# Summing the gathered v rows of a PEER expert layer on TensorE in four 32-column tiles instead of on VectorE

## The chip, the core and the metric

The kernel runs on one core of one Trainium2 chip. The metric is the device time of one execution in microseconds (us). A core has TensorE (PE in the profile, with its weight loads as PEld), VectorE (DVE), ScalarE (ACT), GpSimd (POOL) and SyncE (SP), which issues most transfers. PSUM is the memory that TensorE writes into, in eight banks.

## The reference

One decoder layer on 512 tokens of 1024 channels: a gated mixer of a short convolution and a differential attention, a cross-attention to 256 positions, and then the part that matters here, product-key expert retrieval (PEER): each token and head picks 16 of 16,384 experts, each expert being one row u and one row v.

```python
def chunk(hc):                                     # PEER_HEADS 8, PEER_TOPK 16
    ...
    g = jax.nn.softmax(top_s, axis=-1)
    ue = peer_u[experts]
    ve = peer_v[experts]
    act = jax.nn.gelu(jnp.einsum('td,thkd->thk', hc, ue).astype(jnp.float32), approximate=False)
    return jnp.einsum('thk,thkd->td', (g * act).astype(ve.dtype), ve)
...
x = x + peer_ffn(hf, w_pq[l], sub_keys[l], peer_u[l], peer_v[l])
return rmsnorm(x, final_g)
```

So each token has 128 chosen experts (8 heads by 16), here called its slots.

## The kernel before

Most products run as three float32r passes over a two-part split (hi by hi, hi by lo, lo by hi; `product`, L120). The expert layer takes tokens in two ways. The last 384 tokens (the dense ones) are multiplied with all 16,384 experts, 128 experts to a block j: `stage_u` forms a block's activations (24 matmuls of 384 columns, L120, then a Gelu on ScalarE, L695), and a step of `experts` sums a block up (18 matmuls of 512 columns, L750, into six PSUM banks that stay taken to the end). The first 128 tokens take only the rows they chose: `gathered` fetches rows with an indirect transfer, a token on each partition, so that "row" s is slot s of all 128 tokens (512 KB). Rows 0 to 127 are of u: VectorE multiplies each with the token's normed channels and sums up (L801), which gives the slots' weights `wx`. Rows 128 to 255 are of v: VectorE adds each, times its weight, to `acc` (L812).

The order of the work is set by the loop of `experts` over j = 0 to 127 and by a scheduler that orders the instructions of each engine ahead of time. Steps 85 to 116 hold a `stage_u` as well; steps after that and before it hold only the sum. At the end of each step the loop tells the generator `gathered` how many rows to issue: about one in a step without an activation, three in a step with one, none in the last two. The rows that one step issues are used up in the next. So the v rows begin in step 64, and 96 of the 128 fall to the 32 steps with an activation.

What a step's rows hang on:

- the index column of each row is copied by VectorE into a small tile `now` (L798) that takes its turn with the tiles of tag "e"; before, the row's weight is copied there too (L808);
- the transfer is issued by GpSimd (L818) into one of seven row buffers (four in "res", two "oh", one "row");
- SyncE's queue loads the blocks of u and v for the dense tokens (L108, L733).

At the end the four blocks of tokens get the residual, the norm and the write (L764 to L772); block 0 is the gathered one, with `acc` in SBUF.

Of the kernel before, what the change touches and what calls it, by code (L numbers as in the profile page):

```python
"""Hybrid block on one core: gated short conv + differential attention, memory cross-attention, PEER.

Activations are channel-major ([channel, token]) up to the expert layer. Every float32 product runs
as three float32r passes over exact two-part splits (hi*hi + hi*lo + lo*hi). The expert layer takes
the first 128 tokens by gathering the rows they chose, and the other 384 against all experts on the
tensor engine, with the gates laid out densely.
"""
# [7 lines left out]
F32 = mybir.dt.float32  # L15
F32R = mybir.dt.float32r
BF16 = mybir.dt.bfloat16
I32 = mybir.dt.int32
# [5 lines left out]
P = 128  # L24
# [17 lines left out]
# the order of the work  # L42
EARLY = 5  # convolution channels kept beside the chunks
LAG = 1  # heads before the first convolution channels
SOON = 5  # memory weights loaded ahead of the input
PROLOGUE = 96  # blocks of experts activated before the first is summed up
BY_HEAD = 5  # of them, by each head's choice of experts
BY_BLOCK = 3  # and by each block of tokens' gates
FILL = 4  # and at the end of the gates
AHEAD = 11  # blocks activated ahead of the sum after that  # L50
NA = 3  # one-hot rows of four that ScalarE makes
MM = 1  # gate banks taken from the products
X_HEAD = 4  # gathered rows by two heads' choice
X_BLOCK = 3  # and by each block of tokens' gates
XW = 3  # rows in a step with an activation, to one in a step without
LAST = 2  # steps without rows at the end
LAST_J = 2  # blocks summed up token block by token block at the end
# [4 lines left out]
class Block:  # L62
    # tag: (pool, slots)
    TAGS = {
# [26 lines left out]
    def rows(self, name):  # L91
        """a vector on every partition"""
        src = self.a[name]
        return bass.AP(tensor=src.tensor, offset=src.offset, ap=[[0, P], [1, D]])

# [18 lines left out]
    def product(self, out, w, x):  # L114
        """out[c, t] = sum over d of w[d, c] x[d, t]"""
        whi, wlo = w
        for k in range(KC):
            xhi, xlo = x[0][k], x[1][k]
            for p, (ww, xx) in enumerate(((whi, xhi), (whi, xlo), (wlo, xhi))):
                self.nc.tensor.matmul(out, ww[:, k, :], xx, start=(k == 0 and p == 0), stop=(k == KC - 1 and p == 2))  # L120
# [17 lines left out]
    def roots(self, out, acc, n, inv, eps, log=False, bank="tr"):  # L138
        """out[t, i] = 1 / sqrt(inv * sum of squares + eps) of token 128 i + t; acc holds sums by partition"""
# [7 lines left out]
    def inverse_root(self, out, ss, inv, eps, log=False):  # L147
        """1 / sqrt(ss * inv + eps). By log: exp(-log / 2), and a Newton step, where ScalarE holds that table; else three
        Newton steps from the exponent halved in the bits"""
# [16 lines left out]
    def spread(self, r, n, bank="tr"):  # L166
        """the tokens' values along the free dim, on every partition (in PSUM)"""
# [24 lines left out]
    def parameters(self):  # L192
        nc, a, m = self.nc, self.a, self.misc
        nc.vector.tensor_scalar(out=self.g_sub, in0=self.small[:, 56:57], scalar1=1.0 - LAM_INIT, scalar2=None, op0=ALU.mult)
        # lambda = exp(q1.k1) - exp(q2.k2) + init, the same on every partition
# [9 lines left out]
        # relative bias by distance, reversed: entry e stands for distance 511 - e  # L205
# [36 lines left out]
    def diff_head(self, h, x):  # L242
# [4 lines left out]
        # each component's 64 channels on both halves of the partitions: queries as (hi, lo), keys as (hi, hi)  # L247
# [21 lines left out]
        for pair in range(2):  # L269
            # weights of two query blocks, two key blocks to a tile  # L270
            ahi = [self.t("aw", [P, 2, 2 * P], F32R) for _ in range(pair + 1)]
            alo = [self.t("aw", [P, 2, 2 * P], F32R) for _ in range(pair + 1)]
            for qi in range(2):
# [24 lines left out]
                for b in range(pair + 1):  # L298
# [3 lines left out]
                    if m == 1:  # L302
                        # this key block is all in the future of the pair's first query block
# [32 lines left out]
    def gated(self, sg, w_out, y, gate, x):  # L336
        """sigmoid(gate projection) * (y @ w_out)"""
# [7 lines left out]
    def add_and_scale(self, w, y, res, g):  # L345
        """res += y @ w, in place; returns the split of res * g, and the sums of squares by partition"""
# [19 lines left out]
    def memory(self):  # L366
        """keys and values of the cross-attention, to DRAM: the products need no norm, which scales the positions"""
# [5 lines left out]
        # some weights ahead of the input, which the norm needs as a whole  # L373
# [50 lines left out]
    def mem_keys(self):  # L424
        """channel-major: [channel, position] by chunk"""
# [8 lines left out]
    def mem_values(self):  # L434
        """token-major: [position, part, position block, channel] by chunk"""
# [62 lines left out]
    def keys_scores(self, h, x, yk, xk):  # L498
        """the best 16 keys of each half, for the dense and for the gathered tokens"""
# [15 lines left out]
    def keys_pairs(self, n, vals, idx, ei, ej, ez):  # L515
        """the best 16 sums of one from each half, for n pairs of a head and a block of tokens: rows, columns, sums less the largest"""
# [420 lines left out]
```

## Time and profile before

| | |
|---|---|
| runs of the kernel before | 2159.32 and 2159.57 us, median 2159.45 |
| span of the profiled execution, first to last instruction | 2152.3 us |
| the profiled execution's own time | not recorded apart from its span; the runs are 7.1 us above the span |
| TensorE busy | 2048.0 us, 95% of the span |
| VectorE busy | 1505.0 us, 70% |
| ScalarE busy | 1004.1 us, 47% |
| bytes moved | 440.09 MB, mean 204 GB/s |

The span is cut below into the stretches that matter: from 1714.6 us (step 64, the first v rows) to 1808.7 (step 85), to 1848.8 (step 90), to 2084.4 (step 118), to 2129.5 (step 127), and to the end. The borders are starts of L739, which each step has once on VectorE. Matmuls overlap one another in the trace, so their cost is read from the distance of their starts, not from their durations.

### The profile page before, as it was taken

Reading aid. Unit: us, or ns where it says so; the run is one execution under the profiler, and the core shown is the slowest. Engines: PE = TensorE matmul, PEld = TensorE weight load, DVE = VectorE, ACT = ScalarE, POOL = GpSimd, SP = SyncE. Lnnn points to the kernel's source line nnn. Section 1 sums busy time; section 2 is a strip of 40 time slices with the busy share of each in tenths; the row PEclk is TensorE's granted clock in tenths of the full one; section 3 lists DMA queues with packets and bytes.
Section 4 is the critical chain, followed back from the end, with each engine's and each line's share of the span. In section 5 each row is a group of like instructions: output and inputs, shape, how many; then the busy total and the mean of one; then the engine's idle time right before and its main releaser. Section 6 shows DMA issues by size and latency. Waiting matters only on the chain.

```text
span 2152.3 us, 29167 instructions
## 1 busy us (share of the span) xinstructions
PE 2048.0 (95%) x10341; PEld 1772.6 (82%) x10341; DVE 1505.0 (70%) x3531; ACT 1004.1 (47%) x1716; POOL 341.4 (16%) x301
## 2 busy tenths in 40 slices
PE   7499999999999999999998999999999999999997
PEld 6477877788887878899898989988777877888985
DVE  5356565642345568999887777557887887887897
ACT  5244444432233344343369999953333333333332
POOL 1000000000000000001231111012222234564431
PEclk9799999999999999999999999999999999999999
DMA  7532222223433124246687777589999988899984
GB/s 219 135 98 74 74 85 78 69 88 98 145 110 100 60 78 127 87 129 219 206 281 273 266 279 244 194 299 307 350 321 333 340 310 276 312 357 352 350 298 157
DMA packets 162787, 440.09 MB, mean 204 GB/s; under 512 B 15185, under 2 KB 70497, under 8 KB 160593
## 3 DMA queue, kind: packets, MB, share of 16 engines
q1 hardware_dynamic: 124464, 300.98, 41.7%
q0 software_dynamic: 38176, 137.25, 18.6%
q8 instruction: 81, 1.33, 0.2%
q14 instruction: 66, 0.53, 0.1%
HBM read 391.50 MB, written 46.66 MB: 204 GB/s over the span
## 4 chain that ended last, share of the span: by engine, by line
PE 51%; DMA 13%; DVE 13%; ACT 12%; issue 7%; POOL 2%; another core or an unknown queue 2%; SPq 0%; ACTq 0%; DVEq 0%; POOLq 0%
PE psmm L120 30%; PE psmm L750 5%; ACT slot L858 5%; PE pslg L120 5%; PE pstr L750 4%; DVE lo L99 3%; DMA raw<-in_peer_v 3%; DMA res<-in_peer_v,e 3%; ACT sq L850 3%; DMA act<-sp 2%; ACT hi L98 2%; PE pspv L750 2%; DMA res<-in_peer_u,e 1%; DMA res<-in_peer_u,kp 1%
## 5 line engine op out<-in xcount | busy, mean ns | idle before, releaser
L98 ACT ACTIVATE hi<-raw 128x1024 fp32r<-128x1024 f32 x388 | 410.9, 1061 | 633.0 <-PE psmm L120 288.4
L99 DVE TENSOR_TENSOR lo<-raw,hi 128x1024 fp32r<-128x1024 f32 x388 | 472.7, 1220 | 302.4 <-ACT hi L98 296.1
L120 PE MATMUL psmm<-A,hi 128*128 128x512 f32 x1408 | 451.1, 397 | 1.9 <-DVE Yb L450 1.9
L120 PE MATMUL psmm<-n,hi 128*128 128x384 f32 x1472 | 391.4, 343 | 1.2 <-ACT sp L695 1.2
L120 PEld LDWEIGHTS psmm<-A,hi 128*128 128x128 f32 x1408 | 262.3, 188 | 60.0 <-issue 4.2
L120 PE MATMUL psmm<-A,lo 128*128 128x512 f32 x704 | 280.6, 399 | 0.0
L120 PEld LDWEIGHTS psmm<-n,hi 128*128 128x128 f32 x1472 | 266.7, 188 | 1.6 <-ACT sp L695 1.5
L120 PE MATMUL psmm<-n,lo 128*128 128x384 f32 x736 | 251.6, 342 | 4.7 <-DVE lo L99 4.5
L818 POOL DMA_INDIRECT res<-in_peer_u,e x85 | 94.1, 1107 | 453.9 <-DVE e L798 430.2
L120 PEld LDWEIGHTS psmm<-A,lo 128*128 128x128 f32 x704 | 132.7, 189 | 28.6 <-issue 2.0
L98 ACT ACTIVATE tr<-e 128x384 fp32r<-128x384 f32 x128 | 66.6, 520 | 182.9 <-DVE e L739 179.0
L120 PE MATMUL pslg<-n,hi 128*128 128x384 f32 x576 | 148.3, 338 | 0.0
L120 PEld LDWEIGHTS psmm<-n,lo 128*128 128x128 f32 x736 | 138.3, 188 | 8.2 <-DVE lo L99 7.9
L750 PE MATMUL psmm<-hi,tr 128*128 128x512 f32 x384 | 129.0, 400 | 15.5 <-ACT tr L98 8.5
L801 DVE CUSTOM_DVE_ANT_0 res<-res,hx 128x1024 f32<-128x1024 f32 x101 | 122.5, 1219 | 24.8 <-DMA res<-in_peer_u,e 16.9
L750 PE MATMUL psmm<-lo,tr 128*128 128x512 f32 x384 | 131.1, 396 | 0.3 <-DVE lo L99 0.3
L818 POOL DMA_INDIRECT res<-in_peer_v,e x74 | 103.7, 1401 | 125.2 <-DVE e L808 103.1
L750 PE MATMUL psmm<-hi,e 128*128 128x512 f32 x384 | 119.6, 397 | 1.7 <-DVE e L798 1.6
L818 POOL DMA_INDIRECT res<-in_peer_u,kp x16 | 20.4, 1274 | 616.5 <-DVE kp L798 552.7
L120 PEld LDWEIGHTS pslg<-n,hi 128*128 128x128 f32 x576 | 105.3, 188 | 3.1
L856 DVE TENSOR_SCALAR oh<-iota,e 128x128 f32<-128x128 f32 x384 | 106.8, 345 | 0.0
L812 DVE SCALAR_TENSOR_TENSOR acc<-res,e,acc 128x1024 f32<-128x1024 f32 x73 | 93.5, 1281 | 15.8 <-DMA res<-in_peer_v,e 15.6
(299 smaller groups left out, 3748.2 us busy)
## 6 DMA issues: line engine op xcount, KB each, us to landing
raw<-in_uT SPq DMA_DIRECT2D x128, 512.0 KB, 4.5
raw<-in_peer_v SPq DMA_DIRECT2D x128, 512.0 KB, 5.9
raw<-in_w_in SPq DMA_DIRECT2D x64, 512.0 KB, 3.5
gates<-slot SPq DMA_DIRECT2D x16, 1536.0 KB, 6.7
slot<-gates SPq DMA_DIRECT2D x16, 1536.0 KB, 12.2
act<-sp SPq DMA_DIRECT2D x64, 192.0 KB, 3.8
raw<-in_w_pq SPq DMA_DIRECT2D x16, 512.0 KB, 3.5
raw<-in_w_ckv SPq DMA_DIRECT2D x12, 512.0 KB, 7.5
```

The lines of the kernel that those rows point to most:

```text
L98: self.nc.scalar.activation(hi, src, AF.Copy)
L99: self.nc.vector.tensor_tensor(out=lo, in0=src, in1=hi.bitcast(F32), op=ALU.subtract)
L120: self.nc.tensor.matmul(out, ww[:, k, :], xx, start=(k == 0 and p == 0), stop=(k == KC - 1 and p == 2))
L750: nc.tensor.matmul(accs[2 * i + half], l[:, ts], m[:, half * 512 : half * 512 + 512], start=(jj == 0 and p == 0), stop=(jj == NK - 1 and p ...
L801: nc.vector.tensor_tensor_reduce(out=t, in0=t, in1=hx, op0=ALU.mult, op1=ALU.add, scale=1.0, scalar=0.0, accum_out=wx[:, 0, s : s + 1])
L812: nc.vector.scalar_tensor_tensor(out=acc, in0=t, scalar=w, in1=acc, op0=ALU.mult, op1=ALU.add)
L818: nc.gpsimd.indirect_dma_start(out=t, out_offset=None, in_=a["peer_u"] if s < P else a["peer_v"], in_offset=bass.IndirectOffsetOnAxis(ap=i ...
L850: nc.scalar.activation(sq[:, w, :], self.iota, AF.Square, bias=it[:, t0 + w : t0 + w + 1], scale=-1.0)
L856: nc.vector.tensor_scalar(out=oh[:, 4 + w, :], in0=self.iota, scalar1=cols[:, 0, t - b * TB : t - b * TB + 1], scalar2=cols[:, 1, t - b * ...
L858: nc.scalar.copy(stage[:, :, q * 4 : q * 4 + 4].rearrange("p j w -> p w j"), pp.rearrange("p (w j) -> p w j", w=4))
```

## The change

The 128 v rows are fetched by token: row 128 + k now holds, on partition s, the v row of slot s of token k. The expert indices are transposed once for that (`ext`). The sum over the slots becomes a sum over partitions, so a matmul can do it: for token k the stationary operand is a 128 x 32 block that holds the token's 128 weights in column k mod 32 and zeros elsewhere (`wd`, a tile of 32 such blocks, whose diagonals VectorE refreshes once for each 32 tokens), and the moving operand is a quarter of the row, 256 channels. Quarter q goes to PSUM partitions 32 q to 32 q + 31, so the four matmuls of a token use four column tiles, 32 columns wide, of the array. All operands are float32. 32 tokens accumulate in one bank of tag "lg", which ScalarE then copies to `acc`. The result lies by quarters (partition 32 q + k mod 32), and `gathered_out` finishes block 0 in that layout. The row buffers are six instead of seven, since the buffer "row" now holds `wd`. The change also strips comments, which is left out here.

```diff
-        wx = self.t("wx", [P, 2, P])
-        ex = self.t("ex", [P, P], I32)
-        acc = self.accx = self.t("acc", [P, D])
-        nc.vector.scalar_tensor_tensor(out=ex, in0=xi, scalar=float(NK), in1=xj, op0=ALU.mult, op1=ALU.add)
+        wx = self.t("wx", [P, P])
+        ex, exf = self.t("ex", [P, P], I32), self.t("wt", [P, P])
+        acc = self.accx = self.t("acc", [P, NT, 256])
+        nc.vector.scalar_tensor_tensor(out=exf, in0=xi, scalar=float(NK), in1=xj, op0=ALU.mult, op1=ALU.add)
+        nc.vector.tensor_copy(ex, exf)
+        pt = self.ps("tr")[:, :P]
+        nc.tensor.transpose(pt, exf, self.ident)
+        ext = self.t("xt", [P, P], I32)
+        nc.vector.tensor_copy(ext, pt)
...
-                    nc.vector.tensor_copy(now[:, s - done : s - done + m], ex[:, s % P : s % P + m])
+                    nc.vector.tensor_copy(now[:, s - done : s - done + m], (ex if s < P else ext)[:, s % P : s % P + m])
...
                 else:
-                    w = fl[:, k : k + 1]
-                    nc.vector.tensor_copy(w, wx[:, 1, s - P : s - P + 1])
-                    if s == P:
-                        nc.vector.tensor_scalar(out=acc, in0=t, scalar1=w, scalar2=None, op0=ALU.mult)
-                    else:
-                        nc.vector.scalar_tensor_tensor(out=acc, in0=t, scalar=w, in1=acc, op0=ALU.mult, op1=ALU.add)
+                    k = s - P
+                    b, r = divmod(k, 32)
+                    if wt is None:
+                        wd = self.t("row", [P, 32, 32])
+                        nc.gpsimd.memset(wd, 0.0)
+                        diag = bass.AP(tensor=wd.tensor, offset=wd.offset, ap=[list(wd.ap[0]), [33, 32]])
+                        pt = self.ps("lg")[:, :P]
+                        nc.tensor.transpose(pt, wx, self.ident)
+                        wt = self.t("wt", [P, P])
+                        nc.scalar.copy(wt, pt)
+                    if r == 0:
+                        nc.vector.tensor_copy(diag, wt[:, k : k + 32])
+                        pv = self.ps("lg")[:, :256]
+                    for q in range(4):
+                        nc.tensor.matmul(pv[32 * q : 32 * q + 32, :], wd[:, r, :], t[:, 256 * q : 256 * q + 256], start=(r == 0), stop=(r == 31))
+                    if r == 31:
+                        nc.scalar.copy(acc[:, b, :], pv)
...
-        for i in range(NT):
+        self.gathered_out(fin)
+        for i in range(1, NT):
...
+    def gathered_out(self, fin):
+        nc, a = self.nc, self.a
+        quarters = lambda dram, q: dram.rearrange("(b r) d -> r b d", r=32)[:, :, 256 * q : 256 * q + 256]
+        acc = self.accx
+        xt = self.t("raw", [P, NT, 256])
+        fg = self.t("row", [P, 256])
+        src = a["final_g"]
+        for q in range(4):
+            qs = slice(32 * q, 32 * q + 32)
+            nc.sync.dma_start(out=xt[qs], in_=quarters(self.x3[0], q))
+            nc.sync.dma_start(out=fg[qs], in_=bass.AP(tensor=src.tensor, offset=src.offset + 256 * q, ap=[[0, 32], [1, 256]]))
+        nc.vector.tensor_tensor(out=xt, in0=xt, in1=acc, op=ALU.add)
+        nc.scalar.activation(acc, xt, AF.Square)
+        ss = self.t("sq", [P, 8])
+        nc.vector.tensor_reduce(out=ss[:, 0:4], in_=acc, op=ALU.add, axis=AX.X)
+        quads = self.t("oh", [P, P])
+        nc.sync.dma_start(out=quads, in_=a["quads"])
+        pt = self.ps("lg")[:, :4]
+        nc.tensor.matmul(pt, quads, ss[:, 0:4], start=True, stop=True)
+        self.inverse_root(fin, pt, 1.0 / D, EPS)
+        for b in range(NT):
+            nc.vector.scalar_tensor_tensor(out=xt[:, b], in0=xt[:, b], scalar=fin[:, b : b + 1], in1=fg, op0=ALU.mult, op1=ALU.mult)
+        for q in range(4):
+            nc.sync.dma_start(out=quarters(a["out"][0], q), in_=xt[32 * q : 32 * q + 32])
...
-        self.tags = ("oh", "oh", "row")
+        self.tags = ("oh", "oh")
```

The order of the instructions on TensorE in a step with an activation, where its product (L120) ends and its sum (L750) begins. `pslg` is the bank of the product, `psmm` one of the six banks of the sum. Before:

```order
L120 MATMUL pslg_17409<-n_6485,hi_17412 128x384
L120 MATMUL pslg_17409<-n_6486,hi_17412 128x384
L120 MATMUL pslg_17409<-n_6485,lo_17413 128x384
L750 MATMUL psmm_13138<-hi_17444,tr_17450 128x512
L750 MATMUL psmm_13139<-hi_17444,tr_17450 128x512
```

And in the changed kernel, in such a step (`row` is `wd`; `oh` and `res` are row buffers; `pslg_17476` is the bank of the 32 tokens):

```order
L120 MATMUL pslg_17564<-n_6485,hi_17567 128x384
L120 MATMUL pslg_17564<-n_6486,hi_17567 128x384
L120 MATMUL pslg_17564<-n_6485,lo_17568 128x384
L855 MATMUL pslg_17476<-oh_13182,row_15458 32x256 x3
L855 MATMUL pslg_17476<-oh_13183,row_15458 32x256 x4
L855 MATMUL pslg_17476<-res_7675,row_15458 32x256 x4
L750 MATMUL psmm_13144<-hi_17679,tr_17685 128x512
L750 MATMUL psmm_13145<-hi_17679,tr_17685 128x512
```

The three rows of a step stand between the product and the sum, four matmuls each (one of the twelve stands ahead of the product in this step). Over the whole program the 512 matmuls of L855 stand in 75 unbroken runs between matmuls of the full array: 21 in steps without an activation up to step 85, 45 in the steps with one, 9 in the steps after them.

On VectorE, one step of the same stretch, before (`lo` and the second `e` of L99 are lower halves of splits, L739 lays the gates on, `e` of L798 and L808 is `now`):

```order
L798 COPY e_17696<-ex_7677 128x3
L808 COPY e_17696<-wx_7676 128x1 x3
L739 TENSOR_TENSOR e_17746<-B_16916,slot_17664 128x384
L99 TENSOR_TENSOR lo_17561<-raw_17558,hi_17560 128x1024
L812 SCALAR_TENSOR_TENSOR acc_7678<-res_7675,e_17696,acc_7678 128x1024
L99 TENSOR_TENSOR lo_17593<-raw_17590,hi_17592 128x1024
L812 SCALAR_TENSOR_TENSOR acc_7678<-res_7675,e_17696,acc_7678 128x1024
L99 TENSOR_TENSOR e_17749<-e_17746,tr_17748 128x384
L812 SCALAR_TENSOR_TENSOR acc_7678<-oh_13176,e_17696,acc_7678 128x1024
```

And one in the changed kernel:

```order
L832 COPY e_17384<-xt_7684 128x3
L739 TENSOR_TENSOR e_17440<-B_16524,slot_17192 128x384
L99 TENSOR_TENSOR lo_17325<-raw_17322,hi_17324 128x1024
L99 TENSOR_TENSOR lo_17357<-raw_17354,hi_17356 128x1024
L99 TENSOR_TENSOR e_17443<-e_17440,tr_17442 128x384
```

The three additions to `acc` and the copies of weights are gone, and the index copy reads the transposed indices.

At the end of TensorE's queue the sums of the last two blocks (36 matmuls) stood directly behind the sum of block 125 before. In the changed kernel the last two rows come between:

```order
L750 MATMUL pstr_13148<-hi_19159,e_19166 128x512
L750 MATMUL pspv_13149<-hi_19159,e_19166 128x512
L855 MATMUL pslg_18357<-res_7675,row_15458 32x256 x8
L750 MATMUL psmm_13144<-hi_19196,tr_19202 128x512
L750 MATMUL psmm_13145<-hi_19196,tr_19202 128x512
```

So the last two rows must have landed before the last 36 matmuls start.

## Rows read from the trace of the kernel before

**Rows 1.** The page's part 1: busy time and share of each engine.

```profile
PE 2048.0 (95%) x10341; PEld 1772.6 (82%) x10341; DVE 1505.0 (70%) x3531; ACT 1004.1 (47%) x1716; POOL 341.4 (16%) x301
```

**Rows 2.** Windows from step 64 on: length, then each engine's busy time, clock, DMA.

```profile
core 0: us, PE busy (x) PEld busy (x) DVE busy (x) ACT busy (x) POOL busy (x), PEclk, DMA share, GB/s
1714.60:1808.70 94.10, 90.14 (x381) 71.98 (x380) 74.33 (x131) 32.80 (x44) 30.84 (x21) 0.98 0.86 295
1808.70:1848.80 40.10, 37.25 (x176) 32.54 (x176) 28.75 (x51) 12.01 (x17) 20.91 (x15) 0.96 0.85 299
1848.80:2084.40 235.60, 229.95 (x1144) 207.09 (x1144) 202.75 (x310) 81.38 (x110) 123.18 (x85) 1.00 0.95 343
2084.40:2129.50 45.10, 45.10 (x203) 37.45 (x202) 34.26 (x57) 15.24 (x20) 8.02 (x8) 1.00 0.67 216
2129.50:2152.30 22.80, 9.44 (x40) 6.88 (x38) 18.71 (x72) 6.61 (x18) 0.00 (x0) 0.81 0.25 93
```

**Rows 3.** Timeline of PE, one step: first and last matmuls of product and sum.

```profile
2000.24 0.52 PE L120 MATMUL pslg<-n,hi 128*128 128x384 f32 x2
...
2004.48 0.63 PE L750 MATMUL psmm<-hi,tr 128*128 128x512 f32 x2
...
2008.66 0.51 PE L120 MATMUL pslg<-n,hi 128*128 128x384 f32 x2
```

**Rows 4.** Waits of PE from 1714.6 to 2139 us: total, times, longest.

```profile
PE psmm L750 <- ACT hi L98: 4.1, 2, 2.6
PE pslg L120 <- DVE lo L99: 4.1, 3, 1.7
PE psmm L750 <- ACT tr L98: 3.6, 2, 2.1
PE psmm L750 <- DVE lo L99: 0.3, 1, 0.3
```

**Rows 5.** Line L812 on DVE: counts, ns min/median/max, waits before it.

```profile
L812 DVE SCALAR_TENSOR_TENSOR acc<-res,e,acc x73: 1272/1279/1316, 1731.2 to 2129.9; 128x1024 f32<-128x1024 f32 x73
...
  DMA res<-in_peer_v,e: 15.6, 12
  DMA oh<-in_peer_v,e: 4.3, 4
  DMA row<-in_peer_v,e: 3.1, 4
```

**Rows 6.** Line L808 on DVE, 1848.8 to 2084.4 us: busy, mean ns, idle before.

```profile
L808 DVE COPY e<-wx 128x1 f32<-128x1 f32 x84 | 7.4, 143 | 0.0
```

**Rows 7.** Timeline of PE around L216, a float32 product on a 32 x 32 tile.

```profile
16.94 0.28 PE L120 MATMUL psmm<-head,lo 128*128 128x256 f32 x1
17.06 0.40 PE L120 MATMUL psmm<-head,hi 128*128 128x256 f32 x2
17.39 0.70 PE L216 MATMUL pslg<-rs,vt 32*8 32x320 f32 x2
18.02 0.38 PE L120 MATMUL psmm<-head,lo 128*128 128x256 f32 x1
18.24 0.40 PE L120 MATMUL psmm<-head,hi 128*128 128x256 f32 x2
```

**Rows 8.** Line L216 on PE: ns min/median/max.

```profile
L216 PE MATMUL pslg<-rs,vt x4: 428/430/432, 17.4 to 21.2; 32*8 32x320 f32 x4
```

**Rows 9.** Line L818, the gathers: microseconds from issue to landing.

```profile
DMA to landing us min/median/max: 4.2/7.2/10.6
```

**Rows 10.** ScalarE: Gelu of a product (line L695), a PSUM copy of 256 columns (timeline).

```profile
L695 ACT ACTIVATE A<-pslg x3: 492/492/492, 2004.7 to 2021.5; 128x384 f32<-128x384 f32 x3
...
20.20 0.37 ACT L411 COPY B<-psmm 128x256 f32<-128x256 f32 x1 [0.74 <-PE psmm L120]
```

**Rows 11.** Timeline of the end: the last gather, the last matmul, VectorE's last.

```profile
2125.10 1.07 POOL L818 DMA_INDIRECT res<-in_peer_v,e  x1 [4.98 <-DVE e L808]
...
2138.57 0.40 PE L750 MATMUL pspv<-hi,e 128*128 128x512 f32 x1
...
2147.40 0.16 DVE L164 SCALAR_TENSOR_TENSOR misc<-rt,misc 128x1 f32<-128x1 f32 x1
...
2148.27 0.75 DVE L771 SCALAR_TENSOR_TENSOR hi<-B,misc,hx 128x512 f32<-128x512 f32 x1
```

More of the change, by code (lines that the diff above doesn't have):

```diff
@@ L763, in experts @@
                 nc.sync.dma_start(out=xt[half], in_=self.x3[i][:, sl])
-                nc.vector.tensor_tensor(out=xt[half], in0=self.accx[:, sl] if i == 0 else accs[2 * (i - 1) + half], in1=xt[half], op=ALU.add)
+                nc.vector.tensor_tensor(out=xt[half], in0=accs[2 * (i - 1) + half], in1=xt[half], op=ALU.add)
                 nc.scalar.activation(y[:, sl], xt[half], AF.Square, accum_out=self.misc[:, 28 + 2 * i + half : 29 + 2 * i + half])
@@ L779, in gathered @@
         rows = [rows4[:, k, :] for k in range(4)]
-        wx = self.t("wx", [P, 2, P])
-        ex = self.t("ex", [P, P], I32)
-        acc = self.accx = self.t("acc", [P, D])
-        nc.vector.scalar_tensor_tensor(out=ex, in0=xi, scalar=float(NK), in1=xj, op0=ALU.mult, op1=ALU.add)
+        wx = self.t("wx", [P, P])
[7 more added lines that the diff above has]
+        nc.vector.tensor_copy(ext, pt)
+        wt, pv = None, None
         pend, self.rows_done, used = [], 0, 0
@@ L788, in gathered @@
             upto = done + more
-            if len(rows) == 4 and "row" in self.tags:
+            if len(rows) == 4 and "oh" in self.tags:
                 rows += [self.t(tag, [P, D]) for tag in self.tags]
@@ L793, in gathered @@
             now = self.t(self.turn, [P, 16], I32)
-            fl = now[:, 8:16].bitcast(F32)
             for s in range(done, upto):
@@ L797, in gathered @@
                     m = min(upto, P if s < P else upto) - s
-                    nc.vector.tensor_copy(now[:, s - done : s - done + m], ex[:, s % P : s % P + m])
-            for k, (s, t) in enumerate(pend):
+                    nc.vector.tensor_copy(now[:, s - done : s - done + m], (ex if s < P else ext)[:, s % P : s % P + m])
+            for s, t in pend:
                 if s < P:
-                    nc.vector.tensor_tensor_reduce(out=t, in0=t, in1=hx, op0=ALU.mult, op1=ALU.add, scale=1.0, scalar=0.0, accum_out=wx[:, 0, s : s + 1])
+                    nc.vector.tensor_tensor_reduce(out=t, in0=t, in1=hx, op0=ALU.mult, op1=ALU.add, scale=1.0, scalar=0.0, accum_out=wx[:, s : s + 1])
@@ L802, in gathered @@
                     if s % 16 == 15:
                         sl = slice(s - 15, s + 1)
-                        nc.scalar.activation(wx[:, 1, sl], wx[:, 0, sl], AF.Gelu)
-                        nc.vector.tensor_tensor(out=wx[:, 1, sl], in0=wx[:, 1, sl], in1=xg[:, sl], op=ALU.mult)
-                else:
-                    w = fl[:, k : k + 1]
-                    nc.vector.tensor_copy(w, wx[:, 1, s - P : s - P + 1])
-                    if s == P:
-                        nc.vector.tensor_scalar(out=acc, in0=t, scalar1=w, scalar2=None, op0=ALU.mult)
-                    else:
-                        nc.vector.scalar_tensor_tensor(out=acc, in0=t, scalar=w, in1=acc, op0=ALU.mult, op1=ALU.add)
+                        nc.scalar.activation(wx[:, sl], wx[:, sl], AF.Gelu)
@@ new lines, in gathered @@
+                        nc.vector.tensor_tensor(out=wx[:, sl], in0=wx[:, sl], in1=xg[:, sl], op=ALU.mult)
+                else:
+                    k = s - P
[15 more added lines that the diff above has]
+                        nc.scalar.copy(acc[:, b, :], pv)
@@ L920, in layout @@
     z["buckets"] = _buckets()
+    z["quads"] = np.ascontiguousarray(np.tile(np.eye(32, dtype=f), (4, 4)))
     return z
```

2 rows, old and new, of the table TAGS are left out of this document.

## The prediction

> **What bounds the kernel now.** I read the page's busy shares first, then cut the part that the change touches into windows, and then read what one step costs each engine. The page gives TensorE 95% and VectorE 70% [rows 1], but that is an average over stages; the change touches only step 64 onwards. In the windows from there [rows 2] TensorE is busy 90.1 of 94.1 us, 37.3 of 40.1, 230.0 of 235.6 and 45.1 of 45.1; VectorE 79%, 72%, 86% and 76%. The clock is 0.96 to 1.00 of 2.4 GHz, so there is no slow clock to win back.
>
> A busy TensorE need not be a TensorE at its pace, so I checked one step with an activation [rows 3]: 24 matmuls of 384 columns start 4.24 us apart in sum (0.177 each), 18 of 512 columns 4.18 us (0.232 each), together 8.42 us. The window from step 90 to step 118 holds 28 such steps: 28 x 8.42 = 235.8 us, and it is 235.6 long. So there TensorE's queue of matmuls is the time, with nothing to spare. From 1714.6 to 2139 us TensorE idles 4.0 + 2.9 + 5.6 = 12.5 us in all, and its listed waits are 12.1 us, on splits by ScalarE and VectorE [rows 4]. None is on the additions to `acc`.
>
> **What is taken away.** VectorE loses 128 additions of 1.28 us [rows 5] and 128 weight copies of 0.09 us (7.4 us for 84) [rows 6]: 164 + 11 = 175 us. This lies beside TensorE's matmuls. What it can win is at most the idle 12.5 us; at least nothing. TensorE's waits are on splits, which stand behind additions in VectorE's queue in part, but the longest are on ScalarE's. I take 6 us.
>
> **What TensorE gets.** 128 tokens x 4 matmuls of 256 columns in float32. A float32 matmul shows as two passes: L216 has two matmuls in the program and four in the trace [rows 8]. In the first pair the second pass starts 0.70 - 0.43 = 0.27 us after the first [rows 7, 8], for 320 columns: 2 x 320 / 2.4 GHz is 0.267, so a pass takes two cycles a column. A pass of 256 columns is then 0.27 x 256 / 320 = 0.216 us, and a row has eight of them.
>
> How the passes of four column tiles stand to each other no row of before shows. The bounds: one behind the other, 8 x 0.216 = 1.73 us a row, 221.2 us for 128; all four tiles together, 2 x 0.216 = 0.43 a row, 55.3 us. The nearest row is the pair of L216: the second pass on the same columns waits until the first has streamed. Matmuls leave TensorE's queue in order, so tile 1's first pass can start beside tile 0's second, but not ahead of it, and tile 0's second waits for its first. That is four pass times a row, 0.86 us, with one pass more at the end of each unbroken run: 128 x 0.864 = 110.6, plus 75 x 0.216 = 16.2. I take this value; both ends are kept for the range.
>
> **Leaving the full array and coming back.** L216 stands between matmuls of the full array. Starts before it are 0.12 us apart (16.94, 17.06; the second of the x2 at 17.18). Without L216 the two matmuls behind it would start at 17.30 and 17.42; they start at 18.02 and 18.24 [rows 7]. So 0.82 us were inserted, of which the passes are 0.54, and 0.28 us is the change of tile shape there and back. The order has 75 runs: 75 x 0.28 = 21.0 us.
>
> The Trainium skill (TensorEngine Tiling (Array Packing), section Key Properties) says that a change of the tiling mode drains TensorE, whereas a change of tile within a mode doesn't. It speaks against this change, which breaks the full-array stream 75 times; the 0.28 us agrees. If the kernel had all 128 tokens in one run, by that rule the term would be one switch, and the sum about 37 us less, with the 74 last passes.
>
> **What stands beside this.** The first matmul of a row now waits for its gather, and behind it in TensorE's queue stand all later products and sums; before, only VectorE stood there, and it idled 23.0 us on gathers [rows 5]. A gather lands 7.2 us after issue, 10.6 at worst [rows 9]. With six buffers and three rows a step a buffer has about two steps, over 18 us, from the matmul that frees it to the one that wants it, and its index copy is no longer behind additions in VectorE's queue. So I cost this at 0; without that cover it is up to 23 us. The bytes are the same: 128 rows of 512 KB each way, and longer steps ease a DMA share of 0.95 [rows 2]. SyncE's queue gets a few small transfers more near the end.
>
> The bank that gathers 32 tokens takes one of the two that the products used in turn, so a product now waits for the Gelu of the one before. That takes 0.49 us [rows 10], and 4.18 us of sum lie between; ScalarE is 35% busy there [rows 2]. Cost 0; if ScalarE came late by 0.5 us each time, 32 x 0.5 = 16 us. ScalarE's five copies out of PSUM (0.37 us for 256 columns [rows 10]), VectorE's four of diagonals and GpSimd's one clearing of `wd` lie beside the 4.18 us of sum that the order has between the last token of a bank and the first of the next.
>
> **The ends.** At the start, a float32 transpose and two conversions of 128 columns on VectorE, about 1 us, in a stage where VectorE is the busier. At the end, VectorE finishes 9.7 us after the last matmul starts (2138.57 to 2149.02 less the matmul itself) [rows 11]. Block 0's norm was done before that; now its reciprocal root (12 operations of about 0.16) and four scalings of 256 channels (0.75 for 512, so 0.4) stand ahead of the others': 3.5 us, of which some is won back in the closer packing. I take 3, so 4 us for both ends, bounds 0 and 8. The last two rows stand ahead of the last 36 matmuls (8.4 us); the last gather was issued 13.9 us before TensorE's end and lands about 7 later, so it is just in time.
>
> **The sum.** 110.6 + 16.2 + 21.0 - 6 + 4 = 145.8 us. The profiled execution's span of 2152.3 becomes 2298.1; the runs are 7.1 us above the span, so 2305 us, 6.7% above the median of 2159.45.
>
> **The rivals.**
>
> First, the four tiles run side by side, each with a queue of its own: a row costs 0.432. Then 55.3 + 21.0 - 6 + 4 = 74.3, which is 2234 us. For it: four separate column strips and partitions need nothing of each other. Against it: the second pass of a tile stands ahead of the next tile's first in the queue. The Trainium skill (TensorE: Matmul & The Clock Gate, Part 3, Packing small matmuls) has matmuls on three column tiles at 2.38 times the speed of one after another, and also says that matmuls start and end strictly in program order; no run here shows either. The first would speak for this rival, the second for the forecast.
>
> Second, no overlap at all, that is, the tiles don't do what the change says: 221.2 + 21.0 - 6 + 4 = 240.2, so 2400 us. For it: in every stream read above [rows 3, 7] the starts are a whole matmul's columns apart. Against it: these all use the same columns of the array, which narrow tiles don't.
>
> Third, not slower: within a narrow tile the two passes run beside each other too, so that a row is one pass time, 0.216 us, and the relief of VectorE closes all of TensorE's idle time. 27.6 + 21.0 - 12.5 + 4 = 40.1, so 2200 us, 1.9% above. It decides if a row costs less than 0.24 us. Against it stands the pair of L216, 0.27 us apart. A gain over the kernel before would need matmuls that cost TensorE less than its 12.5 us of idle time, for which I see nothing.
>
> **How the numbers follow.** Chances: the forecast 0.38, side by side 0.28, one after another 0.23, not slower 0.08, and 0.03 for something else. The forecast's own range, with waits on gathers and ScalarE (up to 23 and 16) and the ends, is 2290 to 2345. The range that holds eight in ten reaches from 2215, which takes in side by side, to 2410, which takes in one after another. About 2% (43 us) is what a measurement of this kernel can tell from no change, so 2203 and up counts as slower: 0.90. Within 2%: 0.08. Faster: 0.02.
>
> **What would show it.** Right: starts of L855 in pairs about 0.22 us apart, a row of about 0.86 us, a gap of about 0.28 us more at each change between L855 and L120 or L750, steps with an activation of 8.42 + 3 x 0.86 + 0.5 to 1.0 = 11.5 to 12 us against 8.4, VectorE's share there at half. Wrong: steps under 10.5 us (side by side, 8.42 + 1.3 + 0.3 to 0.6) or near 14; a large wait of PE on gathers, which would mean that the queue and not the arithmetic is the price; or steps that stay near 8.5, by which TensorE would not have been the bound.

## The result, and the profile after

The changed kernel takes 2237.91 us (median of 2236.05 and 2239.77) against 2159.45: ratio 1.0363 with a 95% interval of 1.0333 to 1.0393, 78 us slower. In a second comparison, beside the experiments below, the same two kernels stood at 2229.11 and 2157.70, ratio 1.0347 [1.0315, 1.0378]. The direction was as forecast. The size was that of the first rival (2234), not of the forecast (2305): 2237.91 lies inside the range given, at its lower end, and only because that range had been stretched down to take in this rival; the forecast's own range, 2290 to 2345, missed it.

The profiled execution after has a span of 2234.3 us. Its busy times, to be held against [rows 1]:

```profile
PE 2133.1 (95%) x11369; PEld 1798.7 (81%) x11369; DVE 1355.5 (61%) x3282; ACT 1003.0 (45%) x1718; POOL 300.9 (13%) x302
```

VectorE gave up 150 us and TensorE took on 85. TensorE's 1028 further records are the 512 matmuls of L855 at two passes each, two transposes and the two passes of the product in block 0's norm. The windows from step 64 on, cut at the same steps as [rows 2]:

```profile
1721.80:1822.80 101.00, 101.00 (x528) 71.78 (x527) 49.50 (x90) 31.04 (x43) 25.78 (x21) 1.00 0.78 268
1822.80:1865.20 42.40, 39.67 (x231) 31.63 (x230) 16.24 (x24) 12.63 (x17) 13.32 (x12) 0.96 0.81 275
1865.20:2153.40 288.20, 288.20 (x1840) 229.04 (x1843) 102.03 (x144) 83.39 (x115) 86.98 (x83) 1.00 0.79 277
2153.40:2209.00 55.60, 55.60 (x328) 40.07 (x324) 20.82 (x37) 14.47 (x20) 12.72 (x12) 1.00 0.65 209
2209.00:2234.30 25.30, 10.06 (x54) 7.17 (x46) 19.67 (x74) 6.69 (x16) 0.00 (x0) 0.76 0.28 91
```

Against [rows 2] the five stretches grew by 6.9, 2.3, 52.6, 10.5 and 2.5 us, 74.8 together. The third is the one to look at: 28 steps, three rows each, 10.29 us a step where there were 8.41. TensorE is busy to the last tenth there, VectorE has fallen from 86% to 35%, and the DMA share from 0.95 to 0.79. The other 7.2 us of the longer span had come about before step 64. They aren't the change's: this kernel reached step 64 at 1714.1 in its other profiled execution, and from there to the end it took 513.1 us against 437.7, 75.4 more.

What a row costs can be read from TensorE's timeline of one such step (start, us, engine and line; x8 is one row, x24 three):

```profile
1988.81 0.40 PE L750 MATMUL pspv<-hi,e 128*128 128x512 f32 x1
1989.14 0.64 PE L855 MATMUL pslg<-res,row 128*32 128x256 f32 x8
1989.71 0.62 PE L120 MATMUL pslg<-n,hi 128*128 128x384 f32 x2
...
1993.52 0.52 PE L120 MATMUL pslg<-n,hi 128*128 128x384 f32 x2
1993.88 0.34 PE L120 MATMUL pslg<-n,lo 128*128 128x384 f32 x1
1994.14 1.50 PE L855 MATMUL pslg<-res,row 128*32 128x256 f32 x24
1995.58 0.73 PE L750 MATMUL psmm<-hi,tr 128*128 128x512 f32 x2
1996.15 0.63 PE L750 MATMUL psmm<-lo,tr 128*128 128x512 f32 x2
```

The 24 passes of the second run start at these times (us after 1994, from the trace's records, which are listed in order of time):

```
.142 .149 .156 .162   .382 .389 .396 .402   .598 .605 .611 .618
.814 .821 .827 .834  1.030 1.036 1.043 1.050  1.246 1.252 1.259 1.266
```

They come in fours, 6 to 7 ns apart, and from four to four 0.216 us pass (0.240 the first time). The first passes of all four tiles start together, and then their second passes: a row is 2 x 0.216 = 0.432 us. The change of tile shape is what is left over. Around the single row, from 1988.81 to 1989.71 are 0.90 us where 0.23 would lie between these two without it, and the pair at 1989.71 takes 0.62 instead of 0.52, so 0.77 were inserted, and 0.77 - 0.43 = 0.34. Around the three rows it is 1995.58 - 1993.88 - 0.18 + 0.10 - 3 x 0.432 = 0.32. In the 49 runs of whole rows it is 0.33 to 0.34 in nearly all (median 0.336), whether they hold one row, two, three or five; the other 26 runs hold part of a row and come up below. Taken apart, some 0.10 us of it lie on the way in (from the last full-array matmul to the first pass), 0.02 behind the first passes (0.240 for 0.216), and 0.11 and 0.10 on the way back, ahead of the first full-array matmul and of the second.

TensorE's waits from step 64 to its end, which were 12.1 us [rows 4], are 2.9:

```profile
PE pslg L120 <- ACT B L695: 2.4, 1, 2.4
PE pslg L120 <- DVE lo L99: 0.3, 1, 0.3
PE psmm L750 <- DVE lo L99: 0.2, 1, 0.2
```

None is on a gather. Who waits on the new matmuls is seen at their own line, and at the gathers' line how they land [rows 9]:

```profile
L855 PE MATMUL pslg<-res,row x688: 379/379/403, 1738.3 to 2209.5; 128*32 128x256 f32 x172
...
who waited for it (us, times):
  POOL res L863: 116.9, 20
  POOL oh L863: 83.0, 14
```

```profile
DMA to landing us min/median/max: 4.1/6.4/10.2
```

GpSimd waits 200 us for TensorE to free row buffers before it can issue the next gathers. This costs nothing, since the rows still land before TensorE comes to them. (Of the 1024 passes the trace has all; x688 are those from "res".)

At the end VectorE is last as before [rows 11], with block 0's four scalings (L797) ahead of the other blocks':

```profile
2222.60 1.67 DVE L797 SCALAR_TENSOR_TENSOR raw<-raw,misc,row 128x256 f32<-128x256 f32 x4
...
2229.55 1.41 DVE L772 SCALAR_TENSOR_TENSOR hi<-B,misc,hx 128x512 f32<-128x512 f32 x2
```

### The profile page after: what moved, and what is told of

The parts are those of the page before. It is cut to its first block, busy times and chain, and to the rows that moved or that the text cites. A ratio compares the mean times of both kernels' runs of the same rounds, so it can differ in the third digit from the quotient of the medians.

```text
span 2234.3 us, 31035 instructions
## 1 busy us (share of the span) xinstructions
PE 2133.1 (95%) x11369; PEld 1798.7 (81%) x11369; DVE 1355.5 (61%) x3282; ACT 1003.0 (45%) x1718; POOL 300.9 (13%) x302
## 5 line engine op out<-in xcount | busy, mean ns | idle before, releaser
L99 DVE TENSOR_TENSOR lo<-raw,hi 128x1024 fp32r<-128x1024 f32 x388 | 473.9, 1222 | 370.6 <-ACT hi L98 363.0
L120 PE MATMUL psmm<-A,hi 128*128 128x512 f32 x1408 | 451.1, 396 | 1.9 <-DVE Yb L450 1.9
L120 PE MATMUL psmm<-n,hi 128*128 128x384 f32 x1472 | 392.4, 344 | 1.4 <-ACT sp L695 1.4
L120 PEld LDWEIGHTS psmm<-A,hi 128*128 128x128 f32 x1408 | 262.4, 189 | 60.0 <-issue 4.2
L120 PE MATMUL psmm<-A,lo 128*128 128x512 f32 x704 | 280.6, 399 | 0.0
L120 PEld LDWEIGHTS psmm<-n,hi 128*128 128x128 f32 x1472 | 267.7, 189 | 1.8 <-ACT sp L695 1.8
L120 PE MATMUL psmm<-n,lo 128*128 128x384 f32 x736 | 252.5, 343 | 5.2 <-DVE lo L99 5.0
L99 DVE TENSOR_TENSOR e<-e,tr 128x384 fp32r<-128x384 f32 x128 | 71.1, 555 | 153.4 <-DMA res<-in_peer_v,e 83.3
L120 PEld LDWEIGHTS psmm<-A,lo 128*128 128x128 f32 x704 | 132.6, 188 | 28.7 <-issue 2.0
L120 PE MATMUL pslg<-n,hi 128*128 128x384 f32 x576 | 152.4, 346 | 2.4 <-ACT B L695 2.4
L863 POOL DMA_INDIRECT res<-in_peer_u,e x90 | 102.0, 1133 | 334.0 <-DVE e L832 308.8
L750 PE MATMUL psmm<-hi,tr 128*128 128x512 f32 x384 | 135.4, 410 | 11.9 <-ACT tr L98 8.2
L120 PEld LDWEIGHTS psmm<-n,lo 128*128 128x128 f32 x736 | 138.9, 189 | 8.9 <-DVE lo L99 8.9
L835 DVE CUSTOM_DVE_ANT_0 res<-res,hx 128x1024 f32<-128x1024 f32 x106 | 128.7, 1219 | 23.8 <-DMA res<-in_peer_u,e 15.6
L750 PE MATMUL psmm<-lo,tr 128*128 128x512 f32 x384 | 131.3, 396 | 0.3 <-DVE lo L99 0.2
L863 POOL DMA_INDIRECT res<-in_peer_v,e x86 | 92.4, 1075 | 221.2 <-PE pslg L855 116.9
L750 PE MATMUL psmm<-hi,e 128*128 128x512 f32 x384 | 121.4, 396 | 0.0
L120 PEld LDWEIGHTS pslg<-n,hi 128*128 128x128 f32 x576 | 104.0, 189 | 14.5 <-issue 6.6
## 6 DMA issues: line engine op xcount, KB each, us to landing
slot<-gates SPq DMA_DIRECT2D x16, 1536.0 KB, 12.1
```

What stands on the lines that cost most here:

```text
L99: self.nc.vector.tensor_tensor(out=lo, in0=src, in1=hi.bitcast(F32), op=ALU.subtract)
L750: nc.tensor.matmul(accs[2 * i + half], l[:, ts], m[:, half * 512 : half * 512 + 512], start=(jj == 0 and p == 0), stop=(jj == NK - 1 and p ...
L835: nc.vector.tensor_tensor_reduce(out=t, in0=t, in1=hx, op0=ALU.mult, op1=ALU.add, scale=1.0, scalar=0.0, accum_out=wx[:, s : s + 1])
L863: nc.gpsimd.indirect_dma_start(out=t, out_offset=None, in_=a["peer_u"] if s < P else a["peer_v"], in_offset=bass.IndirectOffsetOnAxis(ap=i ...
```

## The experiments

The theory after the result: TensorE's queue of matmuls is the time, and the change puts into it 128 rows of 0.432 us and 75 runs of 0.33. Its rivals: it is the waits on gathers that TensorE now takes over, the gathers by token or the lost buffer; or the relief of VectorE hides a larger cost.

### One column tile for all four quarters (one_tile)

```diff
...
-nc.tensor.matmul(pv[32 * q : 32 * q + 32, :], wd[:, r, :], t[:, 256 * q : 256 * q + 256], start=(r == 0), stop=(r == 31))
+nc.tensor.matmul(pv[0:32, :], wd[:, r, :], t[:, 256 * q : 256 * q + 256], start=(r == 0 and q == 0), stop=(r == 31 and q == 3))
 if r == 31:
-    nc.scalar.copy(acc[:, b, :], pv)
+    nc.scalar.copy(acc[0:32, b, :], pv[0:32])
```

> All four quarters of a row go to column tile 0 and add up in the same 32 partitions (so the four quarters are summed into one, which is wrong on the other three). If the tiles of the changed kernel run side by side, here the eight passes of 0.216 us follow one another: 1.73 us a row instead of 0.43, 128 x 1.30 = 166 us more, less 3 for 65 runs instead of 75: about 2400 us. If the time of a row is set by something else than by the tiles (its gather, the loads of weights), within 15 us of 2238.

Measured: 2377.28 us, ratio 1.1026 [1.1004, 1.1048]. The timeline of TensorE shows three rows, 24 passes, in 5.3 us:

```profile
2005.75 0.40 PE L750 MATMUL pspv<-hi,e 128*128 128x512 f32 x1
2006.08 5.37 PE L856 MATMUL pslg<-res,row 128*32 128x256 f32 x24
2011.38 0.62 PE L120 MATMUL pslg<-n,hi 128*128 128x384 f32 x2
```

(2011.38 - 2006.08) / 24 is 0.22: the passes follow one another, and a row is 8 x 0.216 = 1.73 us. So the price of a pass in the prediction was right, and the four tiles of the changed kernel do four passes in the time of one. The time is 23 us under the expectation, though. From step 64 to the end the trace has 663.0 us, 150 more than the changed kernel's 512.5: the 166 and the -3 that were expected, and some 11 us less because no row is split between two runs here and TensorE has no wait left (both are costed below).

### All rows of a step through one tile before the next (tile_by_tile)

```diff
+group = []
...
+group.append((r, t))
+if r < 31 and s != pend[-1][0]:
+    continue
 for q in range(4):
-    nc.tensor.matmul(pv[32 * q : 32 * q + 32, :], wd[:, r, :], t[:, 256 * q : 256 * q + 256], start=(r == 0), stop=(r == 31))
+    for rr, tt in group:
+        nc.tensor.matmul(pv[32 * q : 32 * q + 32, :], wd[:, rr, :], tt[:, 256 * q : 256 * q + 256], start=(rr == 0), stop=(rr == 31))
+group = []
```

> The same matmuls as in the changed kernel, but all rows of a step go through tile 0 first, then through tile 1 and so on. If each tile has a queue of its own, a later tile's pass need not wait for the passes of an earlier tile: 2238 us, within 8. If matmuls start strictly in the order of the program, a later tile starts beside the last pass of the tile before: a run of three rows takes 21 pass times instead of 6, that is 3.2 us more in each of about 32 steps with three rows: about 2340 us.

Measured: 2264.0 us, ratio 1.0501 [1.0480, 1.0522]. That is between the two theories, and the timeline says why:

```profile
2002.97 0.33 PE L120 MATMUL pslg<-n,lo 128*128 128x384 f32 x1
2003.24 2.87 PE L860 MATMUL pslg<-res,row 128*32 128x256 f32 x24
2006.04 0.74 PE L750 MATMUL psmm<-hi,tr 128*128 128x512 f32 x2
```

The starts of these 24 passes (us after 2003), sorted into tiles by their even distance of 0.216 (a tile's first pass is told by its 0.403 us; the others have 0.379):

```
tile 0   .238  .478  .694  .910 1.126 1.342
tile 1   .700  .940 1.156 1.372 1.588 1.803
tile 2  1.162 1.402 1.618 1.833 2.049 2.265
tile 3  1.623 1.863 2.079 2.295 2.511 2.727
```

In the program all six passes of tile 0 stand ahead of tile 1's first. Yet tile 1 starts at .700, together with tile 0's third pass and ahead of its fourth. So the starts are not in program order: each tile has a queue of its own. But tile 1 doesn't start at .245 either. It starts when three passes of tile 0 are left to wait, and tile 2 when three of tile 1 are. I read this as queues that hold three passes beside the one that runs (or one matmul beside the one that runs, which these runs can't tell apart, since each matmul has two passes), and a matmul for a full queue holds up those for other tiles. It agrees that steps with two rows, four passes a tile, cost nothing more by this order (1.338 us from the start before to the start behind, against 1.327). One short queue for all tiles doesn't fit: in such a step the four tiles start at 0, 13, 26 and 40 ns, so tile 3 starts past nine passes that still wait, whereas above tile 1 didn't start past the five that waited behind the first. Of the theories neither was right in full: the tiles are independent, over a short distance.

### Only 8 of 256 columns (narrow)

```diff
...
-nc.tensor.matmul(pv[32 * q : 32 * q + 32, :], wd[:, r, :], t[:, 256 * q : 256 * q + 256], start=(r == 0), stop=(r == 31))
+nc.tensor.matmul(pv[32 * q : 32 * q + 32, :8], wd[:, r, :], t[:, 256 * q : 256 * q + 8], start=(r == 0), stop=(r == 31))
 if r == 31:
-    nc.scalar.copy(acc[:, b, :], pv)
+    nc.scalar.copy(acc[:, b, :8], pv[:, :8])
```

> Each of the 512 matmuls of the v rows takes 8 of its 256 columns, and only those are copied out (the other columns of the gathered sum are zero); gathers, waits and runs stay (82 runs instead of 75). If the price is the passes of a row (0.432 us: four tiles side by side, two passes) and the changes of tile shape (0.33 us a run), the passes shrink to something between 0.03 and 0.11 us a row, so 41 to 51 us go: about 2192 us, range 2183 to 2200. If the price is TensorE's queue waiting for gathers, nothing goes: 2232 to 2242.

Measured: 2207.15 us, ratio 1.0241 [1.0223, 1.0258]: 31 us below the changed kernel by the medians, 26 by the ratios to before, but 7 above the range of the theory of prices. What it hadn't counted are waits, 18.9 us where the changed kernel has 2.9:

```profile
PE psmm L750 <- DVE lo L99: 8.9, 6, 3.1
PE psmm L750 <- ACT hi L98: 5.2, 2, 5.0
PE pslg L120 <- ACT B L695: 4.4, 1, 4.4
PE pslg L856 <- DMA res<-in_peer_v,e: 0.4, 1, 0.4
```

Only 0.4 us of that is on a gather, so the theory of waits on gathers falls. The 5.0 us stand behind a split on ScalarE, which itself waited for a block of v to land:

```profile
1989.90 1.06 ACT L98 ACTIVATE hi<-raw 128x1024 fp32r<-128x1024 f32 x1 [7.51 <-DMA raw<-in_peer_v]
...
1991.01 1.65 PE L750 MATMUL psmm<-hi,tr 128*128 128x512 f32 x3 [4.99 <-ACT hi L98]
```

After that wait the matmuls ran slower for a while, as the windows before, during and after show (the clock is the third column from the end):

```profile
1986.00:1991.00 5.00, 0.02 (x3) 0.00 (x0) 0.01 (x1) 1.10 (x2) 0.94 (x1) 0.88 1.03 406
1991.00:1996.40 5.40, 5.39 (x20) 3.86 (x21) 3.31 (x5) 1.39 (x2) 0.94 (x1) 0.50 0.88 291
1996.40:2001.80 5.40, 5.40 (x30) 5.18 (x29) 0.23 (x1) 0.53 (x1) 0.00 (x0) 0.98 0.46 157
```

The granted clock is 0.50, the 1.2 GHz level, after 5.0 us in which TensorE did nothing, and 20 records stand where 30 do at full clock. With shorter rows TensorE ran into a transfer here (DMA share 1.03 in the stretch of the wait); in the changed kernel, with a share of 0.79 in its longer steps, no such wait is left. From step 64 on this trace has 46 us more than that of before: the 82 runs of this order at 0.33 us are 27, the short passes (0.064 us a row) 8, the waits 18.9 - 12.1 = 6.8 and the end 2.5, together 44. So more than half of what the change costs stays when the passes are nearly gone.

### VectorE's additions kept as well (vector_too)

```diff
+nc.vector.scalar_tensor_tensor(out=hx, in0=t, scalar=wt[:, k : k + 1], in1=hx, op0=ALU.mult, op1=ALU.add)
 for q in range(4):
     nc.tensor.matmul(pv[32 * q : 32 * q + 32, :], wd[:, r, :], t[:, 256 * q : 256 * q + 256], start=(r == 0), stop=(r == 31))
```

> The changed kernel, with VectorE's 128 additions of 1.28 us kept as well (into the tile of normed channels, which nothing reads any more). If TensorE's queue is the time, they lie beside it: 2230 to 2250 us (63 runs instead of 75 give 4 back, lost cover takes up to 12). If VectorE's relief is what held the loss to 3.6%, the additions come back as time: 2270 us or more.

Measured: 2243.43 us, ratio 1.0413 [1.0392, 1.0433]; the changed kernel's interval, 1.0333 to 1.0393, just touches this one. By the medians it is 5.5 us more, by the ratios 11. Against the changed kernel's second comparison (1.0347 [1.0315, 1.0378]) it is 14 us more by both, and the intervals lie apart, though 12 runs fewer should have given 4 back. The steps from 90 to 118 take what they take without the additions (285.4 us, 288.2 in the changed kernel), though VectorE is 70% busy instead of 35%:

```profile
1866.90:2152.30 285.40, 283.61 (x1847) 229.58 (x1845) 200.60 (x230) 84.06 (x115) 104.55 (x84) 0.99 0.81 281
```

But TensorE waits again, mostly outside these steps, 14.9 us in all where the changed kernel has 2.9, more than half of it on VectorE's halves of splits:

```profile
PE psmm L750 <- DVE lo L99: 8.4, 4, 4.2
PE pslg L120 <- ACT B L695: 5.5, 1, 5.5
PE pslg L120 <- DVE lo L99: 0.7, 1, 0.7
```

From step 64 to the end this trace has 522.5 us, 10 more than the changed kernel's 512.5. So the first theory holds, with the loss of cover that it allowed for: the additions lie beside TensorE in the long steps and cost some 10 us in all (5.5 to 14 by the comparisons). The relief hides no larger cost.

### VectorE's additions cut short in the kernel before (no_add)

```diff
...
-nc.vector.scalar_tensor_tensor(out=acc, in0=t, scalar=w, in1=acc, op0=ALU.mult, op1=ALU.add)
+nc.vector.scalar_tensor_tensor(out=acc[:, :8], in0=t[:, :8], scalar=w, in1=acc[:, :8], op0=ALU.mult, op1=ALU.add)
```

> The kernel before with VectorE's 128 additions cut to 8 of their 1024 channels (the rest of the sum is left out); gathers and waits stay. It measures what freeing VectorE is worth by itself. If VectorE only follows TensorE, as its 12.5 us of idle TensorE time say, the gain lies between 0 and 12.5 us, more likely under 6, 0.3%. If VectorE's 86% in the steps with an activation hold TensorE back by more than those idle times show, the gain is over 12.5 us, and the change's own cost on TensorE is then larger than the 78 us.

Measured: 2152.04 us against 2157.70, ratio 0.9976 [0.9961, 0.9992], 5.7 us faster (1.7 to 8.4). The additions now take 0.23 us instead of 1.28, in the steps from 90 to 118:

```profile
L813 DVE SCALAR_TENSOR_TENSOR acc<-res,e,acc 128x8 f32<-128x8 f32 x50 | 11.4, 227 | 3.2 <-DMA res<-in_peer_v,e 2.7
```

124 us of VectorE's time taken away (1505.0 to 1380.8 busy) bring some 6 us in the kernel before. Where they lie isn't shown: the profiled execution, one of the longer ones (2154.37), has 437.8 us from step 64 to the end, 437.7 before, and TensorE's waits are 11.8 us where they were 12.1, now mostly on ScalarE's splits:

```profile
PE pslg L120 <- ACT hi L98: 6.9, 2, 5.8
PE psmm L750 <- ACT hi L98: 3.7, 1, 3.7
```

So in that execution TensorE waited as long with the additions nearly gone, and freeing VectorE by itself had little to win.

### The gathers by token, the sum on VectorE (by_token_six)

In the kernel before, with the indices transposed as in the change:

```diff
...
-self.tags = ("oh", "oh", "row")
+self.tags = ("oh", "oh")
...
-nc.vector.tensor_copy(now[:, s - done : s - done + m], ex[:, s % P : s % P + m])
+nc.vector.tensor_copy(now[:, s - done : s - done + m], (ex if s < P else ext)[:, s % P : s % P + m])
```

> The kernel before with two parts of the change alone: the v rows are gathered by token through the transposed indices, and there are six row buffers. VectorE adds them as before (so the sum is over the wrong rows). If the 78 us are TensorE's 512 matmuls and their tile changes, this stands within 0.3% of before (2154 to 2167 us where before has 2159). If the gathers by token or the missing buffer made later landings that the changed kernel pays for, it is slower by 5 us or more, with waits of VectorE on the gathers above the 23 us of before.

Measured: 2157.69 us, ratio 0.9997 [0.9979, 1.0015]. VectorE's waits on the gathers are 26.7 us where they were 23.0 [rows 5]:

```profile
  DMA res<-in_peer_v,e: 19.1, 14
  DMA oh<-in_peer_v,e: 7.6, 6
```

So what the change does to the gathers costs nothing that this can tell, at most 3 us (0.15%) by the interval. The loss lies in the matmuls.

### The same matmuls in fewer runs (threes, again)

```diff
 ends = [int(np.ceil(left * c / sums[-1])) for c in sums] + [left] * LAST
+ends = [e if self.rows_done + e < P else e // 3 * 3 for e in ends]
```

> The changed kernel with v rows handed out only in threes, so that the 512 matmuls stand in 57 unbroken runs instead of 75; the passes, the gathers and the results stay. If each run costs a change of tile shape of about 0.33 us beside its passes (single row in the trace of the changed kernel: 0.766 of cost less 0.432 of passes), 18 runs fewer bring 18 x 0.33 = 6 us, 0.27%: ratio to the changed kernel about 0.997, some 2231 us where it has 2237. If the cost goes with the rows and not with the runs (the 0.77 of a lone row being passes that find nothing beside them), the time stays within 1 us of the changed kernel. A third outcome, later by 2 us or more: the rows of a group of three wait for their gathers, since they are issued together.

> The changed kernel as it is, beside the other kernels of this group and on their chip. Every theory expects its ratio to before again at 1.036, and its distance to the variants of this group is what they are read by.

Measured side by side: threes 2222.76 (ratio 1.0299 [1.0275, 1.0324]), again 2229.11 (1.0347 [1.0315, 1.0378]). The medians are 6.3 us apart; 18 runs fewer at 0.33 are 6.0. The two intervals overlap, so the time alone is not proof, but the traces of both have each kind of run at the same length: a run of five rows takes 2.62 us from the start before to the start behind in both, a run of three 1.76, a single row 0.90. There are 4 single rows left of 30. The cost goes with the runs.

## Why the prediction was right in direction and wrong in size

**TensorE's queue is the time: right.** The window from step 90 to 118 grew by 52.6 us. By the measured prices 28 steps x 3 rows x 0.432 are 36.3 us, their 41 runs x 0.33 are 13.5, and the twelve split rows described below 4.9: 54.7. The 5.7 us that TensorE idled there before [rows 2] are gone, and some 1 us of slow matmuls behind those waits; and as the borders are VectorE's, TensorE got through 23 more of its other matmuls between them, 4.6 us: 52.6. For the same reason the prediction's check came out too well. It set 28 x 8.42 = 235.8 us against a window of 235.6, "with nothing to spare"; TensorE ran 27 products and 27.4 sums in that window and idled 5.7 us.

**The passes of a row: the step that failed.** The prediction took: "Matmuls leave TensorE's queue in order, so tile 1's first pass can start beside tile 0's second, but not ahead of it, and tile 0's second waits for its first." From this came 110.6 us for the rows and 16.2 for the last passes of the runs. The trace shows the four first passes 6 to 7 ns apart and the second passes behind them, so the terms are 55.3 and nothing: 71.5 us too much, more than the whole error of 67. The pair of L216, which the term was read from, has both of its passes on one tile. It tells that a tile takes one pass at a time, which one_tile bears out, and nothing about other tiles. That the queue is a single one, in which a second pass holds up the next tile, was assumed, and tile_by_tile shows that it isn't.

The Trainium skill (TensorE: Matmul & The Clock Gate, Part 3, Packing small matmuls) says that matmuls start and end strictly in program order. In tile_by_tile they don't start so (.700 ahead of .910), and the measurement decides. Another rule, which the prediction didn't weigh, was the better guide: the Trainium skill (TensorEngine Tiling (Array Packing), section Key Properties) has tiles that work independently of each other, each with its loads and matmuls. The trace agrees: 0.432 us a row on four tiles, 1.73 on one.

**The change of tile shape: right in kind, a little small.** 75 x 0.28 = 21.0 was predicted from L216, which shows 32 rows and 8 columns; 0.33 was measured on the 128 x 32 tiles, so 24.8.

**A cost that was not in the sum.** In thirteen places a row's four matmuls are split between two runs, with a product or a sum between, in ten of them with the first matmul alone (one such step is shown in the order of the change, so the sum could have had it):

```profile
2010.37 0.40 PE L750 MATMUL pspv<-hi,e 128*128 128x512 f32 x1
2010.70 0.62 PE L855 MATMUL pslg<-res,row 128*32 128x256 f32 x2
2011.25 0.62 PE L120 MATMUL pslg<-n,hi 128*128 128x384 f32 x2
...
2015.68 1.50 PE L855 MATMUL pslg<-res,row 128*32 128x256 f32 x22
```

The lone matmul costs 0.88 us from the start before to the start behind, as much as a full row (0.90), since the three other tiles stand idle, and the three that are left over cost a row's passes once more. A step with three whole rows in one run takes 10.05 us (products from 1934.93 and 1944.99), one with a lone matmul 10.78 (from 2011.25 and 2022.03). Of the 0.73 between them 0.33 is the further run and 0.4 the split, 5.2 us for thirteen.

**The relief of VectorE: the sign right, the size a guess.** The 6 us were taken from the middle of 0 to 12.5. In the kernel before, no_add gives 5.7 (1.7 to 8.4). In the changed kernel it is more. TensorE's waits fell by 12.1 - 2.9 = 9.2 us, which holds also what the longer steps gave to transfers and splits. By the starts of all matmuls from step 64 on, those behind a wait also come further apart than the 0.176 and 0.231 us of an undisturbed stream: 6.4 us in all before (the granted clock was 0.66 from 1836 to 1841 us, behind a wait of 2.6) and 3.2 after. That is 3.2 more, for which the prediction, with "no slow clock to win back", had no term. vector_too, with the additions back, has 14.9 us of waits.

**What stands beside TensorE: right.** TensorE doesn't wait for a gather (and by_token_six stands at 0.9997). The product's bank made TensorE wait for a Gelu once, for 2.4 us. From the last sum's last matmul to the end of the span are 15.5 us (2218.8 to 2234.3) where 13.7 were (2138.6 to 2152.3): 1.8 more, where 3 was predicted. The rest of the last stretch's 2.5 is the last rows' run. (The 9.7 us that the prediction reads there are 10.05 by its own terms, 10.45 less 0.40; nothing rests on them.)

Together 55.3 + 24.8 + 5.2 - 9.2 - 3.2 + 1.8 = 74.7 us, where the trace has 74.8 from step 64 to the end and the two comparisons 78 and 71. That the first rival's 2234 came so near is in part luck. Its rows are right, but it is 9 us too low by the runs and the split rows, and 8.6 too high by the relief (6 for 12.4) and the ends (4 for 1.8). (The 7.1 us between span and runs, in every sum of the prediction, set two executions of the kernel before against each other; the changed kernel's profiled execution took 2236.05 us with a span of 2234.3, so 1.8.) The chances were 0.38 for the forecast and 0.28 for side by side; with four disjoint sets of columns and one row on a single tile as the only evidence, the trace gave no ground to put the first ahead.

None of the runs points to a version that beats the kernel before: the rows and the runs cost TensorE more than the 6 to 12 us that VectorE's relief is worth, even with passes of 8 columns (35 us in narrow).

## What to carry to other kernels

Ask first whose queue is the time in the stage: here 124 us taken off an engine that was 86% busy were worth some 6 by themselves and 12 beside longer steps, and 0.67 us a row (85.3 for 128) put on the pacing engine made the result. Narrow column tiles do work side by side, so count a group of four as one matmul; but keep them together, interleaved by tile and in few long runs, since each visit to the narrow shape costs 0.33 us and a lone matmul as much as four. Look in the order of the instructions for groups that the scheduler has split. When a term's two bounds lie four times apart and the only row near it doesn't contain the case, give both ends like chances.

## What the runs showed of the hardware that I had not expected

- The two passes of a float32 matmul don't stand in the way of matmuls for other column tiles: four tiles start 6 to 7 ns apart, and 4 x 2 passes of 256 columns take 0.432 us, exactly a quarter of the 1.73 us on one tile.
- With six passes in a row for one tile, the next tile started with its third, 0.46 us after the first; with four passes a tile, all four tiles started within 40 ns. Three waiting passes a tile (or one waiting matmul) is my reading of these groups in tile_by_tile; other sizes were not set out to test it.
- There and back between the full array and 128 x 32 tiles costs 0.33 us, for one row or for five, and about two thirds of it fall on the way back.
- In narrow, 5.0 us without a matmul were followed by 5.4 us at the 1.2 GHz level.
